# A two-layer transformer stack with sparse attention: index scores first, selection and projections spread between attention units

## The chip, the cores and the metric

The kernel runs on one core of a Trainium2 chip. A core has a matrix engine (TensorE, PE in the profile, with its weight loads as PEld), a vector engine (DVE), a scalar engine for activation functions and copies (ACT), a general engine (GpSimd, POOL) and SyncE (SP), which here issues every DMA. Each engine works through its own queue in order; they wait for each other through semaphores. The metric is the device time of one execution in microseconds. Three executions of the kernel before took 2566.44, 2578.88 and 2578.99 us; the median is 2578.88 us.

## The reference

Four layers run one after another on 512 tokens of width 1024 in fp32: a state-space layer, a layer of latent attention, each followed by a feed-forward block, and then two layers of sparse attention, each followed by a gated feed-forward block. The change touches the two sparse layers (a detail of a helper is shared). One of them computes, cut to what matters:

```python
h = x @ w_in                                   # 1024 -> 512 q, 128 k, 128 v, 256+64+4 index, 512 u, 512 vs
logits = einsum('bqhd,bsd->bqhs', qi, ki)      # 4 index heads of 64
score  = einsum('bqhs,bqh->bqs', relu(logits), wi)
score  = where(key_chunk <= query_chunk, score, -inf)
idx    = top_k(score, 128)                     # the 128 best keys of each query
a_out  = softmax(q . k[idx] / 8) @ v[idx]      # 8 heads in 2 key/value groups, 4 blocks of 128 queries
b_out  = gelu(u) * (tril(w_s) @ layer_norm(gelu(vs)) + b_s)
x      = layer_norm(ALPHA * x + concat(a_out, b_out) @ w_o)
```

The feed-forward block and its own layer norm follow.

## The kernel before, in words

**Numbers.** Every product is taken with split operands: a value is copied to a rounded high part, the low part is the difference, and `mm3` (L261 to L267) issues three matmuls for each product. The high part of a weight is made by ACT (L249), the low part by DVE or, inside the sparse layer, by POOL (`lo_eng`, L254). `split` (L121) does the same for activations, with ACT and DVE. Raw weights have two buffers (tag `wr`), split ones five each (`wh`, `wl`), and PSUM has eight banks (`bank`, L86).

**Order of the work.** The program is written out as one long sequence. A planner then orders the instructions of each engine: it takes, from those whose inputs and buffers are ready in its own simulated timeline, the one that was written first. So a later piece may move ahead into a gap of its engine. On the chip the order is fixed.

**Projections.** `tm_gen` (L280) projects all tokens: for each piece of weights (two blocks of 128 input features) it runs the four token tiles, or with `by_token` holds all pieces and runs one token tile after another. A 512-wide projection is 8 input blocks x 4 token tiles x 3 = 96 matmuls of 512 columns. Evacuations put work that needs TensorE again (transposes) into a list `pending`, which `flush` empties one by one between pieces.

**The sparse layer** (`dsa_`, L1437) is written in this order: the index projection (324 columns), the key/value projection (256 columns), index scores for the query tiles t = 1, 2, 3 (L1501 to L1515: four heads each, a relu on ACT and a multiply-add on DVE), the selection (L1519 to L1525), the `vs` projection and its layer norm (`ln_vs`), the `q` projection, the `u` (gate) projection, the attention, the output projection. The selection finds the 128 largest of a row in 16 rounds, each of them a `max` (the eight largest) and a `match_replace` (strike them out), on DVE, over 256, 384 and 512 columns for t = 1, 2, 3; tile 0 needs none.

**Attention.** `attend` (L1218) steps through 32 units, one head and one query tile each: first all heads with query tiles 0 and 1 (16 units, the first half here), then all heads with 2 and 3 (the second half). In a step it issues the scores and the softmax of unit i, one `next` of each filler whose start has come, then the weighting (POOL) and the transposes of unit i-3, and after every second unit the product with the values. Fillers before are `mix` (the spatial gating, from step 0), `turn` (transposes of the gated result, from step 18) and `first` (the first half of the output projection, only after all units). The attention results go straight into `ah`, `al`, the operands of the output projection.

Of the kernel before, what the change touches and what calls it, by code (L numbers as in the profile page):

```python
# [7 lines left out]
F32 = mybir.dt.float32  # L8
# [8 lines left out]
P = 128  # L17
SEQ = 512
# [48 lines left out]
class Net:  # L67
# [212 lines left out]
    def tm_gen(self, wsrc, kts, n, xh, xl, evac, stagger=False, by_token=False, flush=False, done=None):  # L280
# [3 lines left out]
        acc = [self.bank() for _ in range(NT)]  # L284
# [6 lines left out]
        def do(t, piece, off, ks):  # L291
            hi, lo = piece
            for i, kt in enumerate(ks):
                f = seen[t] == 0
                seen[t] += 1
                self.mm3(acc[t][:, :n], xh(kt)[:, t * P:(t + 1) * P], xl(kt)[:, t * P:(t + 1) * P],
                         hi[:, off + i], lo[:, off + i], f, seen[t] == nk)
# [9 lines left out]
        for g in body:  # L307
            for pc, ks in pieces(g):
                for t in range(NT):
                    do(t, pc, 0, ks)  # L310
                if flush:
                    self.flush()
                yield
# [3 lines left out]
        if stagger:  # L317
            for t in range(NT):
                if by_token and t >= 2:
                    self.flush()  # L320
                for pc, ks in ps:
                    do(t, pc, 0, ks)
                evac(t, acc[t])
                if not by_token and len(self.pending) > 2:
                    self.flush()
        else:
            for t in range(NT):
                evac(t, acc[t])
            if done is not None:
                done()  # L330
# [805 lines left out]
    def proj_first(self, wsrc, xh, xl, order=tuple(range(8))):  # L1136
# [6 lines left out]
        return self.tm_gen(wsrc(0), list(order), 512, xh, xl, evac)  # L1143


    def rope(self, dst, src, half, t, c0):
        nc = self.nc
        h = src.shape[1]
        ta = self.tile(self.act, [P, h, 2, half], F32, "a", self.act_bufs)
        tb = self.tile(self.act, [P, h, 2, half], F32, "a", self.act_bufs)  # L1150
# [279 lines left out]
    def dsa(self, *args):  # L1430
        self.lo_eng = self.nc.gpsimd
        with self.phase("dsa") as pool, self.local(16):
            tail = self.dsa_(pool, *args)
        tail()
        self.lo_eng = self.nc.vector

    def dsa_(self, pool, w_in, w_o, gb, sgu_w, sgu_b, sgu_g, sgu_bt):  # L1437
# [17 lines left out]
        score = [self.a() for _ in range(NT)]  # L1455
# [7 lines left out]
        def ev_kv(t, ps):  # L1463
# [4 lines left out]
            for u in range(2):  # L1468
                nc.vector.tensor_copy(y4[:, :, u], y3)
# [11 lines left out]
        with self.phase("idx") as sub:  # L1481
# [18 lines left out]
            self.tm(self.wslab(w_in, 512, 256), list(range(8)), 256, self.Xh, self.Xl, ev_kv, flush=True)  # L1500
            for t in range(1, NT):  # L1501
# [3 lines left out]
                for h in range(4):  # L1505
# [5 lines left out]
                    if h == 0:  # L1511
                        self.ts(s[:, :n], r[:, :n], ws[t][:, 0:1], OP.mult, 0.0, OP.add)
                    else:
                        self.stt(s[:, :n], r[:, :n], ws[t][:, h:h + 1], s[:, :n], OP.mult, OP.add)
                nc.vector.memset(s[0:64, n - 64:n], -2e38)  # L1515

        nc.vector.memset(score[0][:, :P], 0.0)
        nc.vector.memset(score[0][0:64, 64:P], NEG)
        for t in range(1, NT):  # L1519
            s = score[t][:, :(t + 1) * P]  # L1520
            m8 = self.small([P, 8], tag="m8", bufs=8)
            for rnd in range(16):
                nc.vector.max(m8, s)  # L1523
                nc.vector.match_replace(s, m8, s, -3e38)  # L1524
            self.ts(s, s, -2.5e38, OP.is_gt, NEG, OP.mult)  # L1525
        with self.phase("sgu") as sub:
# [4 lines left out]
            self.flush(9)  # L1531
# [11 lines left out]
            def ln_vs():  # L1543
# [3 lines left out]
                self.rsqrt(r, v)  # L1547
                for t in range(NT):
# [19 lines left out]
            self.flush(9)  # L1568
            ah, al = self.fm_x()
# [11 lines left out]
            def turn():  # L1581
                for t in range(NT):
# [7 lines left out]
            def unit(f, g, t, shared):  # L1590
# [15 lines left out]
                if t % 2:  # L1606
                    def pv():
# [3 lines left out]
                        c = slice(t // 2 * 256, t // 2 * 256 + 256)  # L1611
                        self.split(ah[sl, f, c], al[sl, f, c], bk[sl, 0:256])
# [9 lines left out]
            pick = lambda x: (lambda k: x[:, k])  # L1622
            order = list(range(4, 8)) + list(range(4))
            first = self.proj_first(wsrc, pick(ah), pick(al), order)
            self.attend(units, LAG, [(MIX, mix()), (TURN, turn()), (len(units) + 1, first)])


        return lambda: self.proj_ln(wsrc, pick(ah), pick(al), gb, order, first=first)
# [122 lines left out]
```

## Time and profile before

| | us |
|---|---|
| median of three runs | 2578.88 |
| the profiled execution, its own time | 2576.76 |
| its span (first to last instruction) | 2575.0 |
| PE busy | 2445.9 |
| DVE busy | 1601.5 |
| ACT busy | 938.2 |
| POOL busy | 419.8 |

Times in the trace are microseconds from the span's start. The first sparse layer lies at about 1240 to 1482 us, the second at about 1895 to 2137 us. A "busy" PE may run at either of two clocks: a granted clock of 1.00 is 2.4 GHz, 0.50 is 1.2 GHz, and a value between is a mean over a stretch that saw both. The duration of a matmul's row includes its pipeline, so the distance from one start to the next is the time that it costs.

### The profile page before, as it was taken

To read this page: it belongs to the slowest core of one execution; us is meant where nothing else is said; L and a number is where in the kernel's file an instruction comes from. 1 tells how busy PE (TensorE), PEld (TensorE's weight loads), DVE (VectorE), ACT (ScalarE), POOL (GpSimd) and SP (SyncE) were. 2 spreads that over 40 slices of the span, in tenths; PEclk is the share of its full clock that TensorE was granted. 3 is DMA by queue.
4 is the path that set the end of the run, shared out by engine and by line. 5 is a ranking of instruction groups with operands and counts; after the bars stand their busy time and mean duration, and the time that the engine had idled before them with its cause. 6 is when DMAs were issued, how large, how long until landed. Compare 5 with 4: busy or idle time off the path is not lost.

```text
span 2575.0 us, 30661 instructions
## 1 busy us (share of the span) xinstructions
PE 2445.9 (95%) x11961; PEld 2023.6 (79%) x11961; DVE 1601.5 (62%) x2938; ACT 938.2 (36%) x1511; POOL 419.8 (16%) x380
## 2 busy tenths in 40 slices
PE   6799999999989999999898999999989898999998
PEld 5667888888878888888786878888877686888886
DVE  9934366764766566774796563556469646355555
ACT  3223144444245244453334332333323442223331
POOL 6310110001322300001343210000134332000001
PEclk8789999999999999999995999999999689999999
DMA  4224243222321524322420244232133122423211
GB/s 108 56 56 131 82 164 105 91 82 76 97 62 41 176 80 128 104 63 70 131 82 17 82 145 166 66 131 66 60 111 97 33 84 85 167 82 103 94 58 58
DMA packets 182897, 237.55 MB, mean 92 GB/s; under 512 B 19728, under 2 KB 118816, under 8 KB 182688
## 3 DMA queue, kind: packets, MB, share of 16 engines
q1 hardware_dynamic: 182752, 235.59, 28.9%
q8 instruction: 94, 1.54, 0.3%
q14 instruction: 51, 0.42, 0.1%
HBM read 224.56 MB, written 11.01 MB: 91 GB/s over the span
## 4 chain that ended last, share of the span: by engine, by line
PE 81%; DVE 12%; issue 1%; ACT 1%; DMA 0%; POOL 0%; DVEq 0%; ACTq 0%; POOLq 0%
PE ps L265 25%; PE ps L266 24%; PE ps L267 24%; PE ps L127 3%; DVE x L119 3%; DVE a L1524 2%; DVE m L1523 2%; PE ps L784 2%; PE ps L452 1%; PE ps L782 1%; DVE x L109 1%; DVE a L109 1%; DVE vy L109 1%; PE ps L454 1%; DVE a L119 1%
## 5 line engine op out<-in xcount | busy, mean ns | idle before, releaser
L109 POOL TENSOR_TENSOR wl<-wr,wh 128x1024 fp32r<-128x1024 f32 (+4 forms) x124 | 279.4, 2264 | 1817.1 <-ACT wh L249 1133.4
L249 ACT CAST wh<-wr 128x1024 fp32r<-128x1024 f32 (+4 forms) x300 | 305.4, 1021 | 661.9 <-PE ps L267 322.4
L267 PE MATMUL ps<-xh,wl 128*128 128x512 f32 x1248 | 485.4, 389 | 0.6 <-DVE wl L109 0.6
L265 PE MATMUL ps<-xh,wh 128*128 128x512 f32 x1248 | 485.5, 389 | 0.0
L266 PE MATMUL ps<-xl,wh 128*128 128x512 f32 x1248 | 485.5, 389 | 0.0
L109 DVE TENSOR_TENSOR wl<-wr,wh 128x1024 fp32r<-128x1024 f32 x176 | 217.2, 1236 | 225.0 <-ACT wh L249 223.9
L109 DVE TENSOR_TENSOR wl<-wq,wh 128x1024 fp32r<-128x1024 f32 x140 | 170.5, 1221 | 178.1 <-ACT wh L249 177.7
L267 PEld LDWEIGHTS ps<-xh,wl 128*128 128x128 f32 x1248 | 234.3, 188 | 49.5 <-DVE wl L109 1.0
L266 PEld LDWEIGHTS ps<-xl,wh 128*128 128x128 f32 x1248 | 234.3, 188 | 48.6
L265 PEld LDWEIGHTS ps<-xh,wh 128*128 128x128 f32 x1248 | 234.3, 188 | 48.6
L265 PE MATMUL ps<-wh,xh 128*128 128x512 f32 (+4 forms) x704 | 263.2, 377 | 1.8 <-ACT xh L122 1.8
L267 PE MATMUL ps<-wh,xl 128*128 128x512 f32 (+4 forms) x704 | 261.2, 373 | 2.7 <-DVE xl L109 2.7
L266 PE MATMUL ps<-wl,xh 128*128 128x512 f32 (+4 forms) x704 | 260.7, 372 | 0.0
L249 ACT CAST wh<-wq 128x1024 fp32r<-128x1024 f32 x140 | 147.4, 1053 | 284.1 <-PE ps L266 234.5
L266 PE MATMUL ps<-wl,sh 128*128 128x512 f32 x560 | 217.8, 389 | 0.0
L267 PE MATMUL ps<-wh,sl 128*128 128x512 f32 x560 | 217.5, 389 | 0.0
L265 PE MATMUL ps<-wh,sh 128*128 128x512 f32 x560 | 216.9, 389 | 0.0
L267 PEld LDWEIGHTS ps<-wh,xl 128*128 128x128 f32 x704 | 134.7, 192 | 24.0 <-DVE xl L109 3.7
L265 PEld LDWEIGHTS ps<-wh,xh 128*128 128x128 f32 x704 | 135.2, 193 | 22.7 <-ACT xh L122 3.5
L266 PEld LDWEIGHTS ps<-wl,xh 128*128 128x128 f32 x704 | 135.3, 192 | 19.5
L109 DVE TENSOR_TENSOR x<-x,ps 128x512 f32<-128x512 f32 x156 | 103.0, 681 | 73.4 <-PE ps L267 73.2
L109 DVE TENSOR_TENSOR xl<-ps,xh 128x512 fp32r<-128x512 f32 (+2 forms) x128 | 69.3, 553 | 113.8 <-ACT xh L122 108.8
(361 smaller groups left out, 4091.2 us busy)
## 6 DMA issues: line engine op xcount, KB each, us to landing
wr<-in_w_ffn_in_dram SPq DMA_DIRECT2D x44, 1024.0 KB, 5.1
wr<-in_w_ff_dram SPq DMA_DIRECT2D x40, 1024.0 KB, 5.5
wq<-in_w_ff_dram SPq DMA_DIRECT2D x24, 1024.0 KB, 5.2
wq<-in_w_ffn_out_dram SPq DMA_DIRECT2D x16, 1024.0 KB, 8.1
wr<-in_w_in_dram SPq DMA_DIRECT2D x12, 1024.0 KB, 5.3
wr<-in_w_ple_gate_dram SPq DMA_DIRECT2D x8, 1024.0 KB, 5.0
wr<-in_ssm_w_glu_dram SPq DMA_DIRECT2D x6, 1024.0 KB, 5.5
xs<-x SPq DMA_DIRECT2D x24, 256.0 KB, 2.1
```

The lines of the kernel that those rows point to most:

```text
L109: (eng or self.nc.vector).tensor_tensor(out, a, b, op)
L119: (eng or self.nc.vector).scalar_tensor_tensor(out, a, s, b, op0, op1)
L127: self.nc.tensor.transpose(out, in_, self.ident[:k, :k])
L249: self.nc.scalar.copy(hi, src)
L265: mm(ps, lh, rh, start=first, stop=False)
L266: mm(ps, lh, rl, start=False, stop=False)
L267: mm(ps, ll, rh, start=False, stop=last)
L452: self.nc.tensor.matmul(bk[:, c], w[:, kt], self.Xh(kt)[:, c], start=kt == 0 and w is hi, stop=False)
L454: self.nc.tensor.matmul(bk[:, c], hi[:, kt], self.Xl(kt)[:, c], start=False, stop=kt == KD - 1)
L784: nc.tensor.matmul(o, H[sl, r, j], ca[sl, r, j].rearrange("p d c -> p (d c)"), start=False, stop=r == 1)
L1523: nc.vector.max(m8, s)
L1524: nc.vector.match_replace(s, m8, s, -3e38)
```

## The change

Inside the sparse layer the order of the text becomes: index projection, index scores (with the selection of tile 1 right behind its scores), key/value projection, `q` projection, `vs` projection and its layer norm; then the attention. The selection of tiles 2 and 3 becomes a generator, `tops`, of which each step of the attention takes two rounds from step 0. The gate projection becomes a `by_token` generator, `gus`, of which each step takes one part of six matmuls (16 parts). `mix` starts at step 17, `turn` at 20, and of the first half of the output projection eight parts are taken from step 24 on, seven of them with six matmuls. The results of the first half of the units are copied to a new tile `o0`, and `turn` splits it into `ah`, `al`, which are now allocated there. Copies in `ev_kv` and `ev_idx` and the first multiply of the index scores go from DVE to ACT; the normalization in `ln_vs` goes from DVE to ACT and POOL. Score tiles and the rope's temporaries get buffers of their own, and accumulators are allocated when they are first used.

```diff
-    def tm_gen(self, wsrc, kts, n, xh, xl, evac, stagger=False, by_token=False, flush=False, done=None):
+    def tm_gen(self, wsrc, kts, n, xh, xl, evac, stagger=False, by_token=False, flush=False, done=None,
+               fine=False):
...
-        acc = [self.bank() for _ in range(NT)]
+        acc = [None] * NT
...
+            if acc[t] is None:
+                acc[t] = self.bank()
...
                 for t in range(NT):
                     do(t, pc, 0, ks)
+                    if fine:
+                        yield
...
                 for pc, ks in ps:
                     do(t, pc, 0, ks)
+                    if by_token:
+                        yield
                 evac(t, acc[t])
...
-        with self.phase("dsa") as pool, self.local(16):
+        with self.phase("dsa") as pool, self.local(10):
...
+    def top(self, s):
+        m8 = self.small([P, 8], tag="m8", bufs=8)
+        for _ in range(16):
+            self.nc.vector.max(m8, s)
+            self.nc.vector.match_replace(s, m8, s, -3e38)
+            yield
+        self.ts(s, s, -2.5e38, OP.is_gt, NEG, OP.mult)
...
-        score = [self.a() for _ in range(NT)]
+        score = [self.tile(pool, [P, n], F32, f"sc{n}") for n in range(P, SEQ + 1, P)]
+        o0 = self.tile(pool, [P, 4, 256], F32, "o0")
+        A = {}
...
-                nc.vector.tensor_copy(y4[:, :, u], y3)
+                nc.scalar.copy(y4[:, :, u], y3)
...
-                nc.vector.tensor_copy(y[:, 320:384], y[:, 256:320])
+                nc.scalar.copy(y[:, 320:384], y[:, 256:320])
...
-            self.tm(self.wslab(w_in, 512, 256), list(range(8)), 256, self.Xh, self.Xl, ev_kv, flush=True)
+            self.flush(9)
...
-                        self.ts(s[:, :n], r[:, :n], ws[t][:, 0:1], OP.mult, 0.0, OP.add)
+                        nc.scalar.mul(s[:, :n], r[:, :n], ws[t][:, 0:1])
...
+                if t == 1:
+                    for _ in self.top(s[:, :n]):
+                        pass
...
-        for t in range(1, NT):
-            s = score[t][:, :(t + 1) * P]
-            m8 = self.small([P, 8], tag="m8", bufs=8)
-            for rnd in range(16):
-                nc.vector.max(m8, s)
-                nc.vector.match_replace(s, m8, s, -3e38)
-            self.ts(s, s, -2.5e38, OP.is_gt, NEG, OP.mult)
+        def tops():
+            for t in range(2, NT):
+                yield from self.top(score[t][:, :(t + 1) * P])
+        tops = tops()
+        self.tm(self.wslab(w_in, 512, 256), list(range(8)), 256, self.Xh, self.Xl, ev_kv)
...
-                    self.apply([y], mv[:, t, 0:1], r[:, t:t + 1], [sgt[0]], [sgt[1]], [y])
+                    nc.scalar.activation(y, y, AF.Identity, bias=m[:, t:t + 1], scale=r[:, t:t + 1])
+                    self.tt(y, y, sgt[0], OP.mult, nc.gpsimd)
+                    self.tt(y, y, sgt[1], OP.add, nc.gpsimd)
                     nc.scalar.copy(vh[:, t], y)
-                    self.tt(vl[:, t], y, vh[:, t].bitcast(F32), OP.subtract, LNP and nc.gpsimd)
+                    self.tt(vl[:, t], y, vh[:, t].bitcast(F32), OP.subtract, nc.gpsimd)
...
-            self.tm(self.wslab(w_in, 1604, 512), list(range(8)), 512, self.Xh, self.Xl, ev_vs)
+            self.tm(self.wslab(w_in, 0, 512), list(range(8)), 512, self.Xh, self.Xl, ev_q, flush=True)
+            self.tm(self.wslab(w_in, 1604, 512), list(range(8)), 512, self.Xh, self.Xl, ev_vs, flush=True)
+            self.flush(9)
             ln_vs()
-            self.tm(self.wslab(w_in, 0, 512), list(range(8)), 512, self.Xh, self.Xl, ev_q, flush=True)
+            gus = self.tm_gen(self.wslab(w_in, 1092, 512), list(range(8)), 512, self.Xh, self.Xl, ev_gu, by_token=True)
             self.pending.append(finish)
-            self.tm(self.wslab(w_in, 1092, 512), list(range(8)), 512, self.Xh, self.Xl, ev_gu, flush=True)
-            self.flush(9)
-            ah, al = self.fm_x()
...
             def turn():
+                A["h"], A["l"] = ah, al = self.fm_x()
+                self.split(ah[:, 0:4, 0:256], al[:, 0:4, 0:256], o0)
...
-                        self.split(ah[sl, f, c], al[sl, f, c], bk[sl, 0:256])
+                        if t < 2:
+                            nc.scalar.copy(o0[sl, f], bk[sl, 0:256])
+                        else:
+                            self.split(A["h"][sl, f, 256:512], A["l"][sl, f, 256:512], bk[sl, 0:256])
...
-            self.attend(units, LAG, [(MIX, mix()), (TURN, turn()), (len(units) + 1, first)])
+            self.attend(units, LAG, [(0, tops), (0, tops), (0, gus), (17, mix()), (20, turn()), (24, some(first, 8)),
+                                     (len(units) + 2, first)])
```

`proj_first` passes `fine=True` on, `rope` takes its temporaries from a tag of four buffers when it rotates 16 of 64 columns, and `some(gen, n)` passes on the first n parts of a generator.

## Rows read from the trace of the kernel before

**Rows 1.** The page, part 2: granted TensorE clock in 40 equal slices, tenths

```profile
PEclk8789999999999999999995999999999689999999
```

**Rows 2.** Windows by stage, columns from:to, length, busy us (instructions) by engine, clock, DMA

```profile
1272.90:1285.30 12.40, 8.26 (x45) 6.17 (x44) 12.31 (x37) 4.87 (x17) 7.85 (x5) 0.72 0.54 169
1285.30:1354.80 69.50, 68.90 (x315) 56.57 (x313) 69.50 (x196) 25.33 (x42) 32.59 (x15) 1.00 0.25 76
1354.80:1365.00 10.20, 2.19 (x8) 1.68 (x8) 10.13 (x24) 5.27 (x11) 5.29 (x3) 0.58 0.48 105
1365.00:1417.50 52.50, 52.50 (x183) 40.60 (x184) 26.41 (x101) 21.64 (x71) 12.82 (x37) 0.50 0.00 1
1417.50:1438.30 20.80, 20.80 (x127) 16.15 (x127) 14.51 (x45) 13.63 (x36) 7.50 (x20) 0.99 0.38 102
...
2020.50:2073.00 52.50, 52.46 (x183) 40.57 (x184) 26.49 (x102) 21.59 (x71) 12.76 (x37) 0.50 0.00 1
```

**Rows 3.** Timeline of PE: start, duration, instruction, idle time before it and releaser

```profile
1360.25 0.58 PE L265 MATMUL ps<-a,qq 64*128 64x256 f32 x1 [5.47 <-DVE qq L109]
```

**Rows 4.** Windows of 4 us where the granted clock moves, same columns

```profile
1280.00:1284.00 4.00, 3.73 (x17) 2.26 (x15) 4.00 (x19) 1.06 (x4) 0.75 (x1) 0.50 0.66 242
1284.00:1288.00 4.00, 4.00 (x22) 3.47 (x21) 3.96 (x14) 4.00 (x12) 0.76 (x1) 0.90 0.00 0
...
1356.00:1360.00 4.00, 0.00 (x0) 0.00 (x0) 4.00 (x6) 3.10 (x5) 4.00 (x2) 0.56 0.13 24
```

**Rows 5.** Lines of DVE, 1272 to 1440: the selection, 256 columns and value loads

```profile
L1523 DVE MAX8 m<-a 128x8 f32<-128x512 f32 x16 | 10.8, 675 | 0.0
L1523 DVE MAX8 m<-a 128x8 f32<-128x384 f32 x16 | 8.7, 541 | 0.0
L1523 DVE MAX8 m<-a 128x8 f32<-128x256 f32 x16 | 6.5, 408 | 0.0
...
L1524 DVE MATCH_VALUE_LOAD a<-m,a 128x8 f32 x48 | 3.4, 70 | 0.0
```

**Rows 6.** The same view: the copies and the normalization that leave DVE

```profile
L1469 DVE COPY x<-x 128x128 f32<-128x128 f32 x8 | 5.2, 699 | 0.0
...
L119 DVE SCALAR_TENSOR_TENSOR x<-x,mv,x 128x512 f32<-128x512 f32 x4 | 4.6, 1152 | 0.0
...
L119 DVE SCALAR_TENSOR_TENSOR x<-x,vy,x 128x512 f32<-128x512 f32 x4 | 3.8, 995 | 0.0
```

**Rows 7.** Timeline of PE: neighbouring matmuls of 512 and 256 columns at either clock

```profile
1282.14 0.63 PE L267 MATMUL ps<-i,qi 64*128 64x512 f32 x2
1282.57 0.63 PE L265 MATMUL ps<-i,qi 64*128 64x512 f32 x2
...
1347.99 0.39 PE L266 MATMUL ps<-wl,xh 128*128 128x512 f32 x1
1348.22 0.39 PE L267 MATMUL ps<-wh,xl 128*128 128x512 f32 x1
...
1395.47 0.41 PE L267 MATMUL ps<-pt,a 128*128 128x256 f32 x1
1395.68 0.41 PE L265 MATMUL ps<-pt,a 128*128 128x256 f32 x1
...
1420.07 0.28 PE L265 MATMUL ps<-pt,a 128*128 128x256 f32 x1
1420.19 0.28 PE L266 MATMUL ps<-pt,a 128*128 128x256 f32 x1
```

**Rows 8.** Lines of ACT, 1230 to 1440, shapes apart: one load of a function table

```profile
L1192 ACT ACT_TABLE_LOAD x1 | 1.3, 1283 | 0.0
```

**Rows 9.** Lines of POOL, 1272 to 1440: weights' low parts, layer norm's low part

```profile
L109 POOL TENSOR_TENSOR wl<-wr,wh 128x1024 fp32r<-128x1024 f32 x16 | 39.1, 2449 | 36.4 <-ACT wh L249 36.4
...
L109 POOL TENSOR_TENSOR g<-x,g 128x512 fp32r<-128x512 f32 x4 | 5.9, 1516 | 5.0 <-ACT g L1551 5.0
```

**Rows 10.** Timeline of POOL: clearing of probability tiles that the attention's units use

```profile
1238.90 0.64 POOL L430 MEMSET pt<- 128x128 f32 x4
```

More of the change, by code (lines that the diff above doesn't have):

```diff
@@ L1134, in proj_ln, with proj_first @@
             self.tm(wsrc(nh), list(order), 512, xh, xl, ev, stagger=nh == 1)
-    def proj_first(self, wsrc, xh, xl, order=tuple(range(8))):
+    def proj_first(self, wsrc, xh, xl, order=tuple(range(8)), fine=False):
         self.new_r()
@@ L1142, in evac @@
             self.residual(True)(0)(t, ps)
-        return self.tm_gen(wsrc(0), list(order), 512, xh, xl, evac)
+        return self.tm_gen(wsrc(0), list(order), 512, xh, xl, evac, fine=fine)
     def rope(self, dst, src, half, t, c0):
@@ L1148, in rope @@
         h = src.shape[1]
-        ta = self.tile(self.act, [P, h, 2, half], F32, "a", self.act_bufs)
-        tb = self.tile(self.act, [P, h, 2, half], F32, "a", self.act_bufs)
+        if half == 8:
+            ta, tb = (self.tile(self.act, [P, 8, 2, half], F32, "rp", 4)[:, 0:h] for _ in range(2))
+        else:
+            ta, tb = (self.tile(self.act, [P, h, 2, half], F32, "a", self.act_bufs) for _ in range(2))
         s4 = src.rearrange("p h (u f) -> p h u f", u=2)
@@ L1547, in ln_vs @@
                 self.rsqrt(r, v)
+                m = self.small([P, NT], tag="vm4", bufs=2)
+                self.stt(m, mv[:, :, 0], -1.0, r, OP.mult, OP.mult)
                 for t in range(NT):
                     y = ys[t]
-                    self.apply([y], mv[:, t, 0:1], r[:, t:t + 1], [sgt[0]], [sgt[1]], [y])
+                    nc.scalar.activation(y, y, AF.Identity, bias=m[:, t:t + 1], scale=r[:, t:t + 1])
+                    self.tt(y, y, sgt[0], OP.mult, nc.gpsimd)
+                    self.tt(y, y, sgt[1], OP.add, nc.gpsimd)
                     nc.scalar.copy(vh[:, t], y)
-                    self.tt(vl[:, t], y, vh[:, t].bitcast(F32), OP.subtract, LNP and nc.gpsimd)
+                    self.tt(vl[:, t], y, vh[:, t].bitcast(F32), OP.subtract, nc.gpsimd)
             def ev_q(t, ps):
@@ L1610, in pv @@
                         sl = slice(g * 64, g * 64 + 64)
-                        c = slice(t // 2 * 256, t // 2 * 256 + 256)
-                        self.split(ah[sl, f, c], al[sl, f, c], bk[sl, 0:256])
+                        if t < 2:
+                            nc.scalar.copy(o0[sl, f], bk[sl, 0:256])
+                        else:
+                            self.split(A["h"][sl, f, 256:512], A["l"][sl, f, 256:512], bk[sl, 0:256])
                     u["pv"] = pv
@@ L1621, in dsa_, with some @@
                         units += [unit(f, g, 2 * half + i, shared) for i in range(2)]
-            pick = lambda x: (lambda k: x[:, k])
+            pick = lambda x: (lambda k: A[x][:, k])
             order = list(range(4, 8)) + list(range(4))
-            first = self.proj_first(wsrc, pick(ah), pick(al), order)
-            self.attend(units, LAG, [(MIX, mix()), (TURN, turn()), (len(units) + 1, first)])
-        return lambda: self.proj_ln(wsrc, pick(ah), pick(al), gb, order, first=first)
+            first = self.proj_first(wsrc, pick("h"), pick("l"), order, True)
+            def some(gen, n):
+                for _ in range(n):
+                    next(gen, None)
+                    yield
+            self.attend(units, LAG, [(0, tops), (0, tops), (0, gus), (17, mix()), (20, turn()), (24, some(first, 8)),
+                                     (len(units) + 2, first)])
+        return lambda: self.proj_ln(wsrc, pick("h"), pick("l"), gb, order, first=first)
     def swiglu(self, p, w_in, w_out, w_ple, w_pg, gb, final):
```

1 line of the change is left out of this document (removed).

## The prediction

> **What bounds the kernel now.** I read the page's slices first. TensorE is busy nearly everywhere, but the row of its granted clock has two hollows, slices 23 and 31 [rows 1]: they are the two sparse layers. So I cut the first of these layers into stages and asked for busy time and clock in each [rows 2]. The reader is to see five things. (a) From 1272.9 to 1285.3, where the index scores are made, PE is busy for 8.26 of 12.4 us at a mean clock of 0.72, and DVE for 12.31. (b) From 1285.3 to 1354.8 three projections run dense at full clock, while DVE has not a moment free (69.50 of 69.50). (c) From 1354.8 to 1365.0 PE has 2.19 us of work in 10.2; the timeline says what it waits for, a DVE instruction, 5.47 us long [rows 3], and DVE was still in the selection. (d) In that wait the clock fell to 1.2 GHz [rows 4], and it stays at 0.50 for the next 52.5 us, although PE is busy in every one of them. (e) Then the second half of the attention runs at 0.99. The second layer repeats it: its low stretch is 52.50 us long as well [rows 2].
>
> So the bound is not one engine. DVE, loaded with the selection, sets (a) and (c); what (c) leaves behind, a slow clock, sets (d). All terms below are for one sparse layer and count twice.
>
> **The change part by part.**
>
> *The selection leaves the path.* Its cost on DVE: 10.8 + 8.7 + 6.5 = 26.0 us of `max`, about the same for `match_replace` (both pass over the same columns), and 3.4 us of value loads [rows 5], 55 us by durations; starts overlap a little, so some 50. Tile 1's share, a quarter of that, stays ahead of the attention; 37 us may now lie anywhere up to unit 16, the first that needs tile 2. What DVE did besides in (a) to (d) is 12.31 + 69.50 + 10.13 + 26.41 = 118.4 us, selection included [rows 2]. From it go 5.2 us of copies and 4.6 + 3.8 us of normalization [rows 6]: 104.8 us are left. The wait (c) goes: of its 10.2 us, PE's 2.19 at clock 0.58 remain as 1.3, so up to 8.9 us are gained; at worst none, if the first softmax finds DVE as full as before. I take 8, since the rounds of tiles 2 and 3 are now written behind unit 0.
>
> *The index stage (a).* The key/value projection, 96 matmuls of 256 columns at 0.12 us [rows 7], is now written behind the scores and can fill PE's pauses; its evacuation, copies included, no longer stands on DVE ahead of the scores. At full clock the 36 matmuls of the scores cost 12 x (0.12 + 0.17 + 0.23), 6.2 us, with 0.12 and 0.23 from [rows 7] and 0.17 halfway between for 384 columns. With transposes that is 7, so 12.4 could become 7. Bounds: 0 (the eight PSUM banks stay full of scores that DVE has not read) to 5.4. I take 5.
>
> *The clock (d).* If PE does not pause before the attention, the units run at 2.4 GHz. Neighbouring starts show 0.21 us at the low clock against 0.12 for 256 columns, and 0.43 against 0.23 for 512 [rows 7], ratios of 1.75 and 1.9; changes of shape cost more at either clock, so I divide 52.5 by 1.7 and get 30.9: 21.6 us gained. Bounds: 21.6 above. Below, a loss: if the clock stays low, the gate's 96 matmuls, which ran at full clock in (b), are drawn into the slow stretch and pay 96 x 0.2 = 19.2 us. I take the gain, because 512-column work brought the clock from 0.50 to 0.90 within the windows at 1280 and 1284 [rows 4], and each unit now carries six such matmuls.
>
> *The gate between the units.* The work is the same 96 x 0.23 = 22 us, only moved; by itself nothing. PE does 30.9 + 22 us there, and DVE's spread rounds are what it covers. Its evacuations are new between the exponentials: gelu and exp use different tables, and each load takes 1.28 us [rows 8]. Four gate tiles mean up to four turns to gelu and back, eight loads, 10.3 us more on ACT. In (d) ACT was busy 21.64 of 52.5 us [rows 2]. In the new stretch of some 53 us it has 22 + 10 and about 7 of weights and evacuations, 39: it fits, and the lag of three units hides a single load.
>
> The Trainium skill's page "ScalarE: Activation LUTs", section "What ACT_TABLE_LOAD costs", adds a drain of 1.38 us to each load, 2.66 us in all. By that the eight cost 21 us and ACT would stand at 50 of 53 us, hardly below its limit. The trace's row has the load alone, 1.28 us.
>
> *Layer norm on ACT and POOL.* Four tokens, two further POOL passes each of about 1.5 us, as the subtraction of the same shape takes [rows 9]: 12 us, and 18 with the subtraction that was there. It lies behind the `vs` projection, and nothing needs it until `mix` at step 17. But POOL's queue is in order: the weighting of the first units waits behind it, and behind that on PE their transposes; PE has the gate's 22 us to run meanwhile. Without this cover the price is up to 18 us. I take 0 here and let the give-back below carry it. The gate's low weight parts (four of 2.45 us [rows 9]) are written before it and can be made during the `vs` projection.
>
> *The output projection's head start.* Seven parts of six matmuls, 42 x 0.23 = 9.7 us, move from behind the units into their second half. There PE was busy 20.80 of 20.80 us [rows 2], so nothing is won: 0. They hold four of eight PSUM banks from step 24; the units' five results per pair share the rest. If that is short, up to 1 us per pair, 8 in all.
>
> *The rest.* `o0` turns eight small subtractions on DVE into one large, about even or a little better. The small copies on ACT, lazily taken banks, the new buffers: 0, with ACT's idle time over them. SyncE issues the same transfers; the `q` slab takes the place of `vs` in its queue, and both have the same size, so no weights are later for PE than some were before.
>
> *What is given back.* With all of this PE owes 144.6 - 5 - 8 - 21.6 = 110 us over (a) to (d), and DVE 104.8 in the same time: 95%. DVE reached 100% in (b), where three independent chains of rounds were ready; with one chain at a time, and units that wait for each other, it will not quite. In the second half of the attention it was 70% busy (14.51 of 20.8). At 100% nothing is lost; at 80% the stretch takes 131 us, a loss of 21. I take 8, near (b), whose row has the same work.
>
> **Sum.** 5 + 8 + 21.6 - 8 = 26.6 us per layer, 53.2 for both. The profiled execution took 2576.76 us, so 2523.6; it lies 2.1 us below the median of the runs, 2578.88, and with that I say 2525.
>
> **The rivals.**
>
> *DVE becomes the bound.* The selection of tile 3 is late at unit 16, PE waits there, and half of the clock's gain is lost in further pauses: 10 us per layer remain, 2559. For it: the 95% above. Against it: `mix`, `turn` and the head start need no selection, and the planner may draw them ahead.
>
> *ACT becomes the bound.* If no load of a table is hidden, because each stands ahead of an exponential that PE waits for, 8 x 1.28 = 10.3 us per layer come on the path: 2546. For it: the loads fall into the stage with the shortest units. Against it: ACT was busy 22 of 52.5 us. By the 2.66 us of the Trainium skill's page "ScalarE: Activation LUTs" (the section named above) it would be 21 us per layer and 2567.
>
> *The clock stays at 1.2 GHz (the other side).* If PE still pauses as long as at 1354.8, say behind POOL's 18 us, the units begin at the low clock; 52.5 us of unbroken work did not raise it before. Then (d) gains nothing and the gate loses 19.2 us; with 5 and 8 gained elsewhere that is 6 us per layer to the bad, 2591 for two, and up to 2608 if the head start's 42 matmuls (42 x 0.2 = 8.4 us) go the same way. It decides from the point where the mixture of units and gate no longer raises the clock. For it: the row of (d). Against it: the rise behind 1280.
>
> *The order is not the text's.* The planner moves work far: tiles that only the attention uses were cleared at 1238.9 [rows 10], before the index projection. If it had put rounds and projections wherever there was room already, a new order of the text would change little, 2579. Against it: (c), where it found nothing to put.
>
> **How the numbers follow.** Chances: forecast 0.52, DVE bound 0.20, ACT bound 0.05, nothing changes 0.08, clock low 0.15. The forecast's own range is 2510 (nothing given back: 69 us) to 2545. The wide one runs from 2498, with the index stage and the attention a little better still, to 2575, which takes in the DVE rival and part of the unchanged one; outside is mainly the low clock. A measurement of this kernel tells about 0.5% (13 us) from no change. Faster by more: 0.52 + 0.05 + 0.17 of the DVE rival, 0.74. Within: 0.08 + 0.03, 0.11. Slower: 0.15.
>
> **What would show it.** Right: the clock's row without the hollows at both sparse layers; no PE wait of 5 us behind DVE ahead of the first softmax; the gate's matmuls at distances of 0.23 us among units; DVE busy over 85% from the index scores to unit 16. Wrong: a granted clock of 0.50 under gate matmuls, a PE wait on the selection at the second half's first unit, eight table loads with exponentials late behind them, or weightings that stand behind the layer norm on POOL. If both hollows are gone and the time is still above 2560, the sum is wrong and not the mechanism.

## The result, and the profile after

The kernel after takes 2540.27 us (median of four runs, 2538.6 to 2542.13), the kernel before 2575.6 us beside it (four runs, 2566.44 to 2578.99): a ratio of 0.9869, with a 95% interval from 0.9839 to 0.9898. The forecast was 2525 us, in a range from 2498 to 2575. Sign and range held; of the 53 us forecast, 35 came. The kernel before scatters more than after: in the larger sets of the later runs it took 2561.72 to 2582.29 us, with medians of 2570.64 to 2572.13, so the gain may be nearer 31 us than 35. The profiled execution of after took 2540.74 us, its span is 2538.7.

On the page of after, the granted clock in 40 slices answers to [rows 1]: both hollows are gone.

```profile
PEclk9789999999999999999999999999999999999999
```

To see where the time went, I cut both kernels at the same events: the first matmul of the index projection, the first exponential of the attention, the last one, the first sigmoid of the feed-forward block. The windows of before, three for each sparse layer (columns as in [rows 2]; in brackets the instructions):

```profile
1241.20:1363.70 122.50, 110.27 (x586) 94.43 (x584) 107.09 (x314) 47.30 (x90) 54.88 (x27) 0.93 0.36 110
1363.70:1438.20 74.50, 73.24 (x308) 56.70 (x309) 42.22 (x149) 36.14 (x109) 20.21 (x56) 0.64 0.12 31
1438.20:1504.70 66.50, 62.06 (x295) 51.24 (x294) 40.09 (x89) 15.61 (x24) 21.62 (x13) 0.97 0.28 93
1896.70:2019.30 122.60, 109.39 (x586) 94.39 (x584) 106.72 (x312) 46.71 (x89) 53.77 (x27) 0.93 0.35 109
2019.30:2093.70 74.40, 73.16 (x308) 56.62 (x309) 42.28 (x148) 36.08 (x109) 20.20 (x57) 0.64 0.10 30
2093.70:2162.80 69.10, 60.01 (x288) 49.90 (x287) 41.70 (x97) 17.36 (x32) 21.53 (x13) 0.93 0.32 107
```

The same six windows of after:

```profile
1239.20:1339.50 100.30, 92.02 (x510) 78.19 (x508) 91.95 (x274) 42.35 (x91) 39.83 (x19) 0.97 0.36 114
1339.50:1435.30 95.80, 92.85 (x472) 72.30 (x473) 43.76 (x160) 59.59 (x138) 51.17 (x76) 0.95 0.19 56
1435.30:1481.80 46.50, 41.78 (x206) 35.41 (x205) 39.59 (x88) 12.18 (x20) 13.38 (x9) 0.96 0.34 106
1873.60:1977.60 104.00, 93.92 (x510) 80.02 (x508) 95.22 (x279) 41.71 (x90) 38.68 (x19) 0.94 0.36 110
1977.60:2076.10 98.50, 91.98 (x463) 70.87 (x463) 42.66 (x152) 59.27 (x138) 51.77 (x76) 0.95 0.12 33
2076.10:2126.70 50.60, 42.58 (x211) 35.65 (x210) 41.84 (x96) 14.52 (x27) 13.25 (x8) 0.90 0.46 161
```

Matmuls moved from the outer windows into the attention, so lengths alone mislead. I take 0.23 us for each that moved [rows 7], an estimate, since nearly all of them are 512 columns wide (156 of those that came to the attention). Ahead of the attention layer 1 lost 76 matmuls, 17.5 us of work, and 22.2 us of time: its own gain is 4.7 us. In the attention 164 more, 37.7 us of work, cost 21.3 us: 16.4 gained. Behind it 89 fewer, 20.5 us, gave 20.0. The same sum for layer 2 gives 1.1, 11.6 and 0.8. That is 20.6 and 13.5 us, against 20.9 and 13.0 between first matmul and first sigmoid; the other 2 us lie outside the sparse layers.

So the gain is the attention's, whose clock went from 0.64 to 0.95, as the term (d) had it. Ahead of the attention, where (a) and (c) were to give 13 us, there came 4.7 and 1.1. The reason shows in one line of after, the `max` of the selection (count, shortest, median and longest in ns, first and last start), and in two windows, from the first round to the first softmax and from there to the first unit that needs tile 2:

```profile
L1450 DVE MAX8 m<-sc x48: 361/542/683, 1265.3 to 1340.1; 128x8 f32<-128x256 f32 x16, 128x8 f32<-128x384 f32 x16, 128x8 f32<-128x512 f32 x16
```

```profile
1264.00:1337.90 73.90, 70.03 (x366) 57.40 (x362) 73.48 (x206) 30.17 (x60) 34.80 (x15) 0.99 0.35 109
1337.90:1377.60 39.70, 36.05 (x167) 27.50 (x167) 16.96 (x84) 30.69 (x69) 28.60 (x37) 0.91 0.08 27
```

The rounds that are written between the units did not run there. Of the `max` instructions all but the last stand ahead of the first softmax, at 1337.86, where DVE is busy for 73.48 of 73.90 us; in the 39.70 us behind it DVE works for 16.96. The planner had drawn the rounds ahead, to where their scores were ready.

What that costs is best seen in layer 2, from the timeline of after (start, duration, engine, line, instruction; in brackets the idle time before it and what ended it) and its windows:

```profile
1922.15 0.27 ACT L122 CAST a<-ps 128x128 fp32r<-128x128 f32 x1 [8.96 <-DVE rp L109]
...
1923.44 2.34 POOL L109 TENSOR_TENSOR wl<-wr,wh 128x1024 fp32r<-128x1024 f32 x1 [9.07 <-ACT wh L249]
1923.62 2.28 DVE L109 TENSOR_TENSOR x<-rp,rp 128x16 f32<-128x16 f32 x2
...
1926.54 0.69 PE L127 MATMUL ps<-ident,x 128*128 128x128 f32 x2 [6.79 <-ACT x L1489]
```

```profile
1920.00:1924.00 4.00, 0.00 (x0) 0.00 (x0) 4.00 (x15) 1.38 (x3) 0.56 (x1) 1.00 0.00 0
1924.00:1928.00 4.00, 1.46 (x5) 1.27 (x6) 4.00 (x12) 1.00 (x4) 4.00 (x3) 0.54 0.00 0
```

ACT waits 8.96 us for a rope of the keys, which stands behind rounds on DVE; the rope's last two instructions, 16 columns each, then take 2.28 us beside a subtraction of POOL; TensorE waits 6.79 us for the copies that it is to transpose, and its clock falls. In layer 1 the same places cost less (1.4 and 1.8 us), and the attention begins with a wait of 2.96 us.

### The profile page after: what moved, and what is told of

Its sections match the earlier page's. It is cut to its first block, busy times and chain, and to the rows that moved or that the text cites. A ratio compares the mean times of both kernels' runs of the same rounds, so it can differ in the third digit from the quotient of the medians.

```text
span 2538.7 us, 30726 instructions
## 1 busy us (share of the span) xinstructions
PE 2411.8 (95%) x11961; PEld 1992.4 (78%) x11961; DVE 1575.9 (62%) x2880; ACT 968.1 (38%) x1563; POOL 434.0 (17%) x396
## 4 chain that ended last, share of the span: by engine, by line
PE 81%; DVE 12%; ACT 2%; issue 1%; DMA 0%; DVEq 0%; POOL 0%; ACTq 0%
PE ps L265 25%; PE ps L266 24%; PE ps L267 24%; PE ps L127 3%; DVE x L119 2%; DVE sc L1451 2%; DVE m L1450 2%; PE ps L791 2%; PE ps L459 1%; DVE x L109 1%; PE ps L789 1%; DVE vy L109 1%; DVE sc L119 1%; DVE st L360 1%; PE ps L461 1%
## 5 line engine op out<-in xcount | busy, mean ns | idle before, releaser
L265 PE MATMUL ps<-wh,xh 128*128 128x512 f32 (+4 forms) x704 | 271.8, 387 | 3.6 <-ACT xh L122 1.8
L127 PE MATMUL ps<-ident,x 128*128 128x128 f32 x576 | 98.9, 292 | 52.5 <-DVE x L119 32.0
```

What stands on the lines that cost most here:

```text
L127: self.nc.tensor.transpose(out, in_, self.ident[:k, :k])
L265: mm(ps, lh, rh, start=first, stop=False)
```

## The experiments

All ratios are to the kernel before, on the same chip; after itself stands at 0.9869. Times in brackets are medians. The interval of a ratio is about 0.002 to 0.003 to either side, so two kernels that differ by less than some 0.003 (8 us) are not told apart by it; the ratio of after also rests on only four runs of before, with a median some 4 us above that of the later sets. "Stage 1" is the window from the index projection's first matmul to the first exponential. For each profiled execution, the length of the sparse layers from that first matmul to the first sigmoid, in us:

| kernel | layer 1 | layer 2 |
|---|---|---|
| before | 263.5 | 266.1 |
| after | 242.6 | 253.1 |
| few_rounds | 241.0 | 238.4 |
| late3 | 235.2 | 249.4 |
| no_pool_lo | 236.2 | 235.3 |
| pool_memset | 238.3 | 240.3 |
| gate_before | 259.1 | 262.7 |
| gate_before_ln | 255.5 | 257.4 |
| before_few | 247.1 | 258.1 |
| before_gate | 251.2 | 255.2 |
| one_gelu | 244.7 | 247.9 |
| ln_dve | 241.3 | 252.0 |
| late3_ln_gelu | 235.6 | 239.0 |
| late3_lod_gelu_ln | 245.0 | 248.8 |

**few_rounds.** The size of the selection.

```diff
-                yield from self.top(score[t][:, :(t + 1) * P])
+                yield from self.top(score[t][:, :(t + 1) * P], 2)   # rounds
```

> The kernel after, with 2 of the 16 selection rounds for the query tiles 2 and 3 (14 rounds of each are left out, 36 us of DVE per layer). Theory A (the rounds that the planner drew ahead of the attention fill DVE there, and PE's pauses before the first softmax stand behind them): about 10 us of pauses and low clock go in each layer, 2518 to 2524 us. Theory B (table loads on ACT and the layer norm on POOL inside the attention are what is left on the path): 2535 to 2540 us.

0.9814 [0.9786, 0.9842] (2523.28 us), in theory A's span. Stage 1 is 88.5 and 87.4 us, 11.8 and 16.6 less than in after; some 5 of it is gate work that now comes later (23 and 22 matmuls). The table shows more than the total: nearly all of the gain is layer 2's. In layer 1 stage 1 gained 6.5 us by the sum above, and the attention lost 4.5 of them again, with 3.0 us of waits behind ACT and a clock of 0.92. So theory A is right on stage 1, but a shorter stage 1 is not a shorter layer by itself.

**late3.** The same rounds, later.

```diff
+            s = score[3]
+            self.stt(s[:, 0:1], A["sum"], 0.0, s[:, 0:1], OP.mult, OP.add)
-            for t in range(2, NT):
-                yield from self.top(score[t][:, :(t + 1) * P])
+            yield from self.top(score[2][:, :3 * P])
+            yield from self.top(s)
```

> The kernel after, with the selection of tile 3 tied to the first unit: one tiny DVE instruction adds 0 times the sum of the first unit's exponentials to its scores, so that the planner can't draw its rounds ahead of the attention. Theory A: DVE has 23 us less ahead of the attention in each layer, and is idle for most of 1344 to 1384 us: 2522 to 2530 us. Theory B: 2538 to 2542 us. Rival (the rounds now delay softmaxes and evacuations, or unit 16 waits for tile 3): above 2545 us.

0.9841 [0.9814, 0.9869] (2529.3 us), within theory A's span, with every round done. Its ratio is 0.0028 under that of after, just short of what the ratio tells; its four runs (2527.24 to 2530.89 us) all lie more than 7 us under the lowest of after. The windows of stage 1 and attention in layer 1, stage 1 in layer 2, and a line of PE's waits in layer 2 (total, times, longest):

```profile
1238.20:1326.70 88.50, 85.66 (x487) 74.69 (x486) 69.82 (x228) 42.11 (x91) 38.99 (x19) 0.97 0.41 127
1326.70:1426.80 100.10, 96.70 (x496) 74.41 (x495) 64.13 (x206) 60.37 (x137) 52.19 (x77) 0.97 0.18 55
1865.00:1964.50 99.50, 86.77 (x488) 75.11 (x487) 73.52 (x228) 42.11 (x91) 38.28 (x19) 0.93 0.36 115
```

```profile
PE ps L127 <- ACT x L1489: 9.6, 1, 9.6
```

Layer 1 has the short stage 1 of few_rounds, and DVE carries the rounds in the attention, where it had been idle (64.13 us busy in place of 43.76). Layer 2 keeps the wait for the keys, now 9.6 us. Why it falls on layer 2 alone stays open.

**no_pool_lo and pool_memset.** DVE beside POOL.

```diff
         self.nc.scalar.copy(hi, src)
-        self.tt(lo, src, hi.bitcast(F32), OP.subtract, eng)      # eng: POOL
+        self.nc.scalar.copy(lo, src)                             # no_pool_lo
+        # pool_memset: ahead of that copy, two times nc.gpsimd.memset(lo, 0.0)
```

> The kernel after, with the low weight parts of the sparse layers made by a copy on ACT in place of the subtraction on POOL (the correction is left out; ACT has one more pass of 1.05 us per piece). Theory C (a DVE instruction with its operands in SBUF stands still while POOL works on SBUF: 12.5 and 13.3 us of DVE's time in the two layers are such excess): the pauses behind ropes and index scores go in part, 2525 to 2533 us. Theory A alone (only the number of rounds counts): 2537 to 2543 us. If ACT's 17 us more per layer matter: above 2545 us.

> As no_pool_lo (low weight parts by a copy on ACT, the correction left out), but POOL keeps about as long a piece of work for each of them, at the same place in its queue: two memsets of the buffer, some 2.3 us, that write SBUF and read nothing; the copy waits for them. Theory C (DVE stands still while POOL works on operands in SBUF): the excess of DVE's instructions stays away, 2510 to 2520 us. Rival Q (POOL's own queue: layer norm and weightings stand behind the weights, low parts come late): the gain of no_pool_lo goes, 2530 to 2542 us.

no_pool_lo came to 0.977 [0.9742, 0.9798] (2510.53 us), more than any theory had; pool_memset to 0.9808 [0.9784, 0.9832] (2518.36 us), where theory C put it. Two forms of DVE's instructions in layer 1 (count, busy us, mean ns), first in after, then in no_pool_lo, then in pool_memset, each with two SBUF inputs; and last, POOL's memsets:

```profile
L109 DVE TENSOR_TENSOR x<-rp,rp 128x16 f32<-128x16 f32 x8 | 5.3, 699 | 0.0
L119 DVE SCALAR_TENSOR_TENSOR sc<-i,wsc,sc 128x512 f32<-128x512 f32 x3 | 5.0, 1658 | 0.0
```

```profile
L110 DVE TENSOR_TENSOR x<-rp,rp 128x16 f32<-128x16 f32 x8 | 0.9, 196 | 0.0
L120 DVE SCALAR_TENSOR_TENSOR sc<-i,wsc,sc 128x512 f32<-128x512 f32 x3 | 2.2, 728 | 0.0
```

```profile
L110 DVE TENSOR_TENSOR x<-rp,rp 128x16 f32<-128x16 f32 x8 | 0.8, 164 | 0.0
L120 DVE SCALAR_TENSOR_TENSOR sc<-i,wsc,sc 128x512 f32<-128x512 f32 x3 | 2.2, 719 | 0.0
```

```profile
L257 POOL MEMSET wl<- 128x1024 f32 x40 | 38.1, 954 | 50.3 <-PE ps L272 36.1 <-PE ps L273 13.2
```

The same small instruction takes 699 ns on the mean beside subtractions on POOL, and 164 beside memsets. The memsets were a little short (1.9 us a pair, where the subtraction takes 2.4), so some of the difference between the two runs may be that; but they fill POOL for 38 us of this stretch, and DVE does not feel them. Of the 0.0099 between after and no_pool_lo, 0.0061 stay in pool_memset: by these ratios some 16 of 25 us, with a doubt of about 10 by their intervals, go with DVE's standing still beside POOL's reads. The rest is what POOL's queue and the later low parts cost; it was not split further.

**gate_before and gate_before_ln.** The gate's place.

```diff
-            gus = self.tm_gen(self.wslab(w_in, 1092, 512), ..., ev_gu, by_token=True)
+            self.tm(self.wslab(w_in, 1092, 512), ..., ev_gu, flush=True)
+            self.flush(9)
...
+                    self.tt(y, y, sgt[0], OP.mult)               # _ln: on DVE, both passes
```

> The kernel after, with the gate projection ahead of the attention again (behind the vs projection, as one dense block); all else stays. Theory D (the gate's 512-column matmuls among the units are what brings the clock up after the pause before the first softmax): the low clock comes back, 20 us per layer lost, 2575 to 2585 us. Rival E (the new order alone does it: the selection has 22 us of dense projection more to hide under, no long pause is left, and the clock needs no gate): 2530 to 2542 us, with 12 table loads less.

> As gate_before (gate projection dense ahead of the attention), with the two passes of the layer norm on DVE in place of POOL. Theory F (the pause of 12.5 us of gate_before stands behind the layer norm on POOL; without it PE doesn't pause and the units keep the clock): pause under 3 us, granted clock near 1.00 in the units, 2535 to 2546 us. Theory D (the units by themselves do not hold the clock, the gate's matmuls do): the clock is at 0.50 for some 30 us per layer also here, 2552 to 2560 us.

0.9973 [0.9958, 0.9988] (2563.99 us) and 0.9942 [0.9924, 0.9959] (2554.73 us). First a wait of PE in layer 1 of gate_before, and its attention:

```profile
PE ps L127 <- POOL x L116: 12.5, 1, 12.5
```

```profile
1360.40:1448.10 87.70, 81.01 (x377) 62.55 (x378) 38.65 (x133) 40.06 (x113) 33.84 (x65) 0.78 0.16 49
```

Then the same of gate_before_ln:

```profile
PE ps L127 <- POOL x L116: 8.3, 1, 8.3
```

```profile
1359.00:1443.10 84.10, 81.35 (x377) 62.85 (x378) 38.71 (x133) 39.36 (x112) 28.73 (x62) 0.79 0.17 51
```

In both the clock of the attention is down again (before: 0.64, after: 0.95), as theory D had it: in layer 1 it stays at 0.50 from 1358.5 to 1399.5 and from 1357.4 to 1394.9, in after for 6.8 us behind the first softmax. By the sum above, the attention of layer 1 gains 2.7 and 6.3 us on before, where after gains 16.4. The time of gate_before lies in neither theory's span, 11 us under theory D's; that of gate_before_ln lies in theory D's. Theory F was not put to a clean test: with the layer norm's passes on DVE a pause of 8.3 us is left, since the first exponential comes at 1359.0 only and POOL has the norm's subtractions and weights ahead of the weightings. So neither run shows whether units without a pause ahead of them would keep the high clock. The waits show a second thing that the gate does: it gives PE work while the weightings stand behind the layer norm.

**before_few.** The same question put to the kernel before.

```diff
-            for rnd in range(16):
+            for rnd in range(16 if t == 1 else 2):
```

> The kernel before, with 2 of the 16 selection rounds for the tiles 2 and 3 (14 rounds of each left out). Step (c) and (d) of the prediction (the wait ahead of the first softmax is the selection's, and the low clock is the wait's): the wait of 5 us and the low clock of 52 us go in both layers, 8 + 21.6 us each, 2510 to 2530 us. Rival (the wait is also that of other DVE and ACT work, and the clock stays low behind a shorter one): 2555 to 2570 us.

0.992 [0.9891, 0.9949] (2547.67 us), neither span. Windows of before_few around the first exponential of layer 1, at 1354.9 us:

```profile
1352.00:1354.00 2.00, 1.41 (x10) 1.02 (x9) 0.96 (x4) 1.98 (x5) 1.36 (x1) 1.00 1.08 225
1354.00:1356.00 2.00, 0.90 (x6) 0.49 (x5) 0.79 (x3) 1.87 (x4) 1.30 (x2) 1.00 0.57 104
1356.00:1360.00 4.00, 4.00 (x23) 3.50 (x24) 3.94 (x15) 1.64 (x7) 0.62 (x3) 0.80 0.00 0
1360.00:1396.00 36.00, 36.00 (x123) 26.90 (x122) 16.28 (x71) 15.03 (x53) 9.66 (x30) 0.50 0.00 1
```

The long wait is gone; 1.7 us of pauses are left. The clock falls all the same and stays at 0.50 for 36 us in which PE is never idle; in layer 2 it does so for 51.2 us (1996.7 to 2047.9). So the length of the wait (c) was not what kept the clock low, and the units of tiles 0 and 1 by themselves did not bring it back. The short pauses stand just ahead of the fall, so that units would run at 1.2 GHz with no pause at all is not shown.

**before_gate.** The gate among the units, with what has to move with it (`mix`, `turn`, `o0`).

```diff
-            self.tm(self.wslab(w_in, 1092, 512), ..., ev_gu, flush=True)
-            self.flush(9)
-            ah, al = self.fm_x()
+            self.flush(9)
+            gus = self.tm_gen(self.wslab(w_in, 1092, 512), ..., ev_gu, by_token=True)
...
-            self.attend(units, LAG, [(MIX, mix()), (TURN, turn()), (len(units) + 1, first)])
+            self.attend(units, LAG, [(0, gus), (17, mix()), (20, turn()), (len(units) + 1, first)])
```

> The kernel before with one part of the change alone: the gate projection as a filler of the attention's steps (with what it needs: mix from step 17, turn from step 20, the tile o0). Order of the index scores, selection, layer norm and head start stay as before. Theory D (the gate's 512-column matmuls among the units bring the clock back, whatever pause is ahead of them): busy time at the low clock in the attention falls from 53 us to 10 to 15 per layer, 16 to 18 us gained in each, 2536 to 2546 us, most of the whole change. Rival G (the selection has 22 us of dense projection less to hide under, so the wait ahead of the first softmax grows by as much and eats the gain): 2560 to 2580 us.

0.9931 [0.9913, 0.9949] (2552.55 us), half of the change, between the two spans. Stage 1 and attention of its layer 1, and two windows from the start of that attention:

```profile
1241.00:1346.10 105.10, 89.39 (x482) 77.39 (x481) 89.67 (x283) 38.80 (x76) 39.32 (x19) 0.89 0.35 108
1346.10:1426.30 80.20, 79.81 (x405) 59.97 (x404) 51.59 (x170) 55.84 (x130) 34.83 (x62) 0.92 0.19 51
...
1344.00:1352.00 8.00, 8.00 (x20) 5.42 (x20) 8.00 (x21) 4.68 (x8) 3.54 (x3) 0.50 0.00 0
1352.00:1360.00 8.00, 8.00 (x21) 5.44 (x21) 6.23 (x23) 2.27 (x4) 2.73 (x3) 0.52 0.00 0
```

Both theories have a part of it. The attention takes 80.2 us with 97 matmuls more than before's 74.5, at a clock of 0.92: by the sum above it gains 16.6 us (14.7 in layer 2), no less than in after. But stage 1 loses 6.5 us by the same sum: it has 15.7 us without PE (before: 12.2), as rival G had it, and the clock is already down in it. Nor does the gate bring the clock back at once: with PE busy throughout, gate and units together run at 0.50 for 13.5 us in the attention of layer 1 and 17.3 in layer 2, within or just above theory D's 10 to 15.

**one_gelu and ln_dve.** ACT's table loads, POOL's layer norm.

```diff
-                nc.scalar.activation(gu[:, t], ps, AF.Gelu_apprx_tanh)
+                nc.scalar.copy(gu[:, t], ps)       # one_gelu; one gelu over gu at the start of mix
...
-                    self.tt(y, y, sgt[0], OP.mult, nc.gpsimd)
+                    self.tt(y, y, sgt[0], OP.mult)   # ln_dve; the same for the add
```

> The kernel after, with the gate copied from PSUM by ACT (no table needed) and one gelu over all four tiles ahead of the spatial gating: 16 table loads in the program in place of 24. Theory B1 (the loads are on the path): 8 x 1.28 = 10.3 us less, some 2 of them given back for the added pass, 2530 to 2534 us. Rival (they are hidden by the lag of three units): 2538 to 2542 us.

> The kernel after, with the layer norm's multiply and add by the parameters (two passes of four tiles) on DVE in place of POOL. Theory B2 (weightings of units stand behind the layer norm in POOL's queue, PE pauses at 1988 us and the clock falls): 2533 to 2537 us. Rival (DVE is still in the selection when the layer norm comes, the 5.5 us per layer go on the path): 2543 to 2552 us.

0.9869 [0.9849, 0.9888] (2536.95 us) and 0.9868 [0.9848, 0.9888] (2536.58 us): neither is told from after by the ratio. The time of one_gelu lies between the spans of theory B1 and its rival: of the 10.3 us of eight loads the medians show 3, in sets of runs taken apart, and the ratio shows nothing. The time of ln_dve lies in theory B2's span, but in its layer 2 the pause has moved and not gone: the clock still falls, at 1987.3, and PE waits 5.03 us, up to 1991.47, for a copy on ACT that stands behind two table loads.

**late3_ln_gelu and late3_lod_gelu_ln.** The edits together, and then the low weight parts on DVE.

```diff
     def dsa(self, *args):
-        self.lo_eng = self.nc.gpsimd      # late3_lod_gelu_ln
```

> late3 with two further edits: the two passes of the layer norm on DVE, and the gate copied from PSUM by ACT (no table needed) with one gelu over all four tiles ahead of the spatial gating, which makes 16 table loads of 24 in the program. Theory B2 (table loads and POOL cost time of their own in the attention, about 4 and 2 us per layer): 2512 to 2520 us. Rival (they lie beside PE's work once the selection is out of the way): 2526 to 2531 us.

> late3_ln_gelu with the low weight parts of the sparse layers on DVE in place of POOL. Theory C: DVE's excess beside POOL (10 us per layer in late3_ln_gelu) goes, for subtractions of 1.22 us, some 15 to 20 of them ahead of the first softmax: 2508 to 2516 us if the tile 3's rounds leave room for them. Rival (DVE becomes the bound of the projections again): 2522 to 2535 us.

late3_ln_gelu: 0.9803 [0.9782, 0.9824] (2518.8 us, four runs from 2518.11 to 2520.04), the fastest kernel here that does all of the work, 2% under before and below every run of after. Stage 1 and attention of its layer 2:

```profile
1866.50:1955.40 88.90, 86.09 (x488) 75.03 (x487) 70.19 (x228) 41.80 (x92) 38.31 (x19) 0.96 0.40 128
1955.40:2054.60 99.20, 96.44 (x484) 74.32 (x483) 67.47 (x214) 56.50 (x133) 43.84 (x69) 0.95 0.12 34
```

The time is in theory B2's span, for another reason: against late3 the attention is only 1 us shorter (99.2 to 100.2, with 12 matmuls fewer), while stage 1 lost 10.6 us, and with them the wait of 9.6 for the keys. No table load stands near that wait in either trace; that the planner found another order is the likely cause, but not shown.

late3_lod_gelu_ln: 0.9866 [0.9847, 0.9886] (2535.3 us), at the upper end of the rival's span, but not by its mechanism. Stage 1 is good (87.7 and 87.2 us); it is in the attention that PE waits for the selection, at the first unit that needs tile 3. A line of its waits in layer 1, and the chain that ended last there:

```profile
PE ps L127 <- POOL x L116: 7.5, 2, 7.1
```

```profile
1382.39 0.67 DVE sc L1450 x2
1383.08 0.44 DVE sc L116
1383.55 0.69 DVE x L1200
...
1385.98 0.70 POOL x L116
1386.73 1.12 PE ps L127 x4
```

The last round ends at 1383, its mask, then the softmax, the weighting, and the transposes that PE waits for: the late selection of the prediction's DVE rival, in a kernel that gave DVE more to do. DVE was not full there (71.03 of 108.30 us); its rounds stood between other work in its queue.

## Why the prediction was right, and where it was not

**The bound** was named half right. DVE did hold stage 1. The clock did fall in the wait (c), but that the wait is what left the slow clock of (d) behind is not borne out: before_few has no long wait and 36 and 51 us at 0.50, and before_gate has longer pauses than before and a clock of 0.92. The 5.47 us of [rows 3] are TensorE's wait, not the length of the DVE instruction it waited for.

**(a) and (c), 13 us per layer: the step that failed.** It was "I take 8, since the rounds of tiles 2 and 3 are now written behind unit 0". The text's order was taken for the chip's. Measured were 4.7 and 1.1 us, for both terms together. The sign "no PE wait of 5 us behind DVE ahead of the first softmax" failed in layer 2, where PE waits 6.79 us for the keys, and they for DVE. With the rounds of tile 3 really late, stage 1 is 88.6 and 88.9 us (late3_ln_gelu), with 98 matmuls less than before's: by the same sum as above 11.4 and 11.2 us are gained, near the 13. The warning stood in the prediction as the rival "the order is not the text's" [rows 10], at 0.08, but only for the whole change, not for this step.

**(d), 21.6 us, with 8 given back: right in size.** 13.6 us were left by the sum, 16.4 and 11.6 came in the attention. That the gate among the units is what raises the clock there, gate_before, gate_before_ln, before_few and before_gate bear out, each from another side. That the width of its matmuls is what counts is not shown: in gate_before the clock came back at 1399.5 behind 4 us of nothing but 256-column matmuls, one transpose apart.

**The give-back** was to come from a DVE at 95% throughout. DVE was at 99% from the first round to the first softmax and at 43% from there to unit 16, 80% over both, so the sign "DVE busy over 85% from the index scores to unit 16" was wrong. What the attention did give back were pauses and short stretches at the low clock; that this came near the 8 us is luck.

**Gate and tables.** The gate's matmuls run at 0.23 us among the units while the clock is up, as two neighbouring starts of after show; behind the pauses (1340.7 to 1347.5 in layer 1) they start 0.43 us apart, the sign "0.50 under gate matmuls" on a small scale:

```profile
2001.62 0.40 PE L265 MATMUL ps<-wh,xh 128*128 128x512 f32 x1
2001.86 0.40 PE L266 MATMUL ps<-wl,xh 128*128 128x512 f32 x1
```

There are six table loads more per layer, not eight, and most are hidden, as priced: two of them (at 1363.76 and 1374.94) lie on the chain that ended last in the attention of layer 1, and one_gelu, with eight fewer in the program, is by its median 3 us faster. By the Trainium skill's page "ScalarE: Activation LUTs", section "What ACT_TABLE_LOAD costs", each would cost 2.66 us with its drain; the trace doesn't agree: the load of the rows below takes 1.28 us, starts 0.02 us behind the end of the instruction ahead of it, and the activation starts at 1988.11, 0.01 us behind the load's end.

**Layer norm on POOL, 0 us, with 18 if the cover is gone: right mechanism.** In layer 2 of after the weighting stands behind it, and PE behind the weighting:

```profile
1983.45 6.24 POOL L109 TENSOR_TENSOR x<-x,x 128x512 f32<-128x512 f32 x5
...
1986.82 1.28 ACT L1556 ACT_TABLE_LOAD   x1
...
1988.11 1.09 ACT L1556 ACTIVATE g<-ps 128x512 f32<-128x512 f32 x2
...
1989.65 1.29 POOL L116 TENSOR_SCALAR x<-x,sm 128x256 f32<-128x256 f32 x3
1990.19 0.44 PE L127 MATMUL ps<-ident,x 128*128 128x128 f32 x2 [2.20 <-POOL x L116]
```

With the gate's matmuls beside it PE loses 2.20 us; without them 12.5 (gate_before).

**Not weighed at all: DVE beside POOL.** The prediction priced DVE's instructions one by one, as if they were independent of POOL's. In the wait (c) of before itself, the selection's mask of 256 columns took 2.07 us on DVE beside POOL; the same mask takes 0.28 in pool_memset.

**Not tried by itself:** the head start, and the copies and the normalization that left DVE.

## What to carry to other kernels

A stretch at the low clock need not end when the pause ahead of it is made shorter: look at what TensorE runs in it, and try independent projection matmuls (here 512 columns wide) as filler among the narrow ones. Where a planner orders the instructions, "written later" is no delay: here only a true dependency was (late3's one tiny instruction), and the order that is built has to be read before a gain is put on it. Before work is counted as free because its engine is idle, compare how long its neighbour's instructions take beside it and without it.

## What the runs showed of the hardware

I had not expected how much DVE stands still beside POOL. I took the lowest tenth of each form's durations in a trace as its own cost, and summed what instructions took beyond it, where that was more than 0.15 us, from the index projection to the last exponential. In before that is 18.6 and 17.8 us in the two layers, in after 11.7 and 12.1, and every such instruction overlaps one of POOL. In no_pool_lo and in pool_memset the sum is 0.0 in both. In after the forms are mostly ropes and score sums, with two operands in SBUF, and some masks. Two such operands are not the only case. In before a large part, 6.8 us over both layers, is that of the small copies (L1469) of [rows 6], which read one: four of the sixteen take 1.0 to 2.3 us, each beside POOL's subtractions or multiplications, and the other twelve 0.21. The mask of 256 columns reads one too: it takes 1.89 and 1.56 us in after and 0.28 in pool_memset. The count misses it, since both of its instances in after are slow, so the sums are from below. `max` and `match_replace` keep their durations (675 and 671 ns for 512 columns in after). The Trainium skill's page "SBUF — State Buffer", section "Who interferes with whom", says that a DVE instruction with two SBUF inputs contends with a POOL instruction that reads SBUF, and not with one that only writes it; 699 ns beside subtractions and 164 beside memsets, for the rope's, agree.
